# Loads of two rows, and half of the row sums with their halves added on TensorE

## The chip, the cores and the metric

The kernel runs on one core of one Trainium2 chip. The metric is the device time of an execution in microseconds. The times before are those of three runs.

## The reference

The input `x` has 32 x 512 rows of 1024 positive fp32 numbers, 67.1 MB in all. For each row the sum of the reciprocals is wanted:

```python
def reference(x: np.ndarray) -> np.ndarray:
    return np.sum(1.0 / x, axis=-1).astype(np.float32)
```

## The kernel before

The 16384 rows are laid out as 128 partitions with 128 rows each (`x_v`), so that "a row" below means one row in each of the 128 partitions: a tile of 128 x 1024 fp32, 512 KB. The kernel walks once over these 128 rows in loads of one to four rows, listed in `GROUPS`. An entry `(np_, ns, eng)` is one load with `np_` paired rows and `ns` single rows; `eng` is the engine that forms the products. All instructions are issued in the order of the list, and each engine works its own queue in that order. There is no planner.

A paired row is worked by its halves a and b, 512 elements each, with 1/a + 1/b = (a + b) / (a b):

- SyncE loads the rows of the group into `xt` (line 73). `xpool` has eight buffers of up to four rows.
- GpSimd multiplies the halves, `pr` = a b (line 75), for all paired rows of the load in one instruction. For the last row VectorE does it.
- ScalarE forms the reciprocal of the product as Exp(-Ln(S pr)) with S = 2^17: Ln in place in `pr` (line 85), and Exp into `rc` in PSUM (line 87), each for all paired rows in one instruction.
- VectorE multiplies the whole row of 1024 by `rc`, which is read twice through a broadcast, and sums into one column of `sums` (line 90), one instruction for each row. The sum of both products is S (a + b) / (S a b).

A single row (the `ns` rows) needs no product: ScalarE takes Ln and Exp(-Ln) of all 1024 elements with a running sum (lines 77 and 78), and neither GpSimd nor VectorE touches it. The list before has 112 paired and 16 single rows: two loads of two rows, then fifteen loads of `(3, 1)` alternating with fourteen of `(4, 0)`, two loads of two rows, and four of one.

When VectorE has read the last row of a load, its `xt` buffer is free, and SyncE may issue the load eight places further on. `pr` has four buffers, `rc` two. At the end `sums` goes out in one transfer (line 103). TensorE does nothing in this kernel.

Of the kernel before, what the change touches and what calls it, by code (L numbers as in the profile page):

```python
# [1 line left out]

# [5 lines left out]


@with_exitstack  # L10
def kernel(
    ctx: ExitStack,
    tc: tile.TileContext,
    x: bass.AP,
    out: bass.AP,
):

    nc = tc.nc
    f32 = mybir.dt.float32
    P = 128
    D = 1024
    H = D // 2
    F = 128

    S = float(2**17)


    GP, DV = nc.gpsimd, nc.vector
    GROUPS = (
        [(1, 1, GP), (2, 0, GP)]
        + [(3, 1, GP), (4, 0, GP)] * 14
        + [(3, 1, GP), (2, 0, GP), (2, 0, GP)]
        + [(1, 0, GP), (1, 0, GP), (1, 0, GP), (1, 0, DV)]
    )  # L40

    Ln = mybir.ActivationFunctionType.Ln
    Exp = mybir.ActivationFunctionType.Exp
    mult = mybir.AluOpType.mult
    add = mybir.AluOpType.add

    x_v = x.flatten_outer_dims().rearrange("(p f) d -> p f d", p=P)
    out_v = out.flatten().rearrange("(p f) -> p f", p=P)

    act_sets = list(get_activation_tables(nc.m.arch).keys())  # L50
    nc.scalar.add_instruction(  # L51
        mybir.InstLoadActFuncSet(
            name=nc.get_next_instruction_name(),
            act_func_set_id=act_sets.index("natural_log_exp_and_others"),
            ins=[],
            outs=[],
        )
    )

    xpool = ctx.enter_context(tc.tile_pool(name="xpool", bufs=8))  # L60
    ppool = ctx.enter_context(tc.tile_pool(name="ppool", bufs=4))
    opool = ctx.enter_context(tc.tile_pool(name="opool", bufs=1))
    rpool = ctx.enter_context(
        tc.tile_pool(name="rpool", bufs=2, space=bass.MemoryType.PSUM)
    )

    sums = opool.tile([P, F], f32)

    c0 = 0
    for np_, ns, eng in GROUPS:  # L70
        n = np_ + ns
        xt = xpool.tile([P, n, D], f32, tag="xt")
        nc.sync.dma_start(out=xt, in_=x_v[:, c0 : c0 + n, :])
        pr = ppool.tile([P, np_, H], f32, tag="pr")
        eng.tensor_tensor(out=pr, in0=xt[:, :np_, :H], in1=xt[:, :np_, H:], op=mult)  # L75
        for j in range(np_, n):
            nc.scalar.activation(out=xt[:, j, :], in_=xt[:, j, :], func=Ln)  # L77
            nc.scalar.activation(  # L78
                out=xt[:, j, :],
                in_=xt[:, j, :],  # L80
                func=Exp,
                scale=-1.0,
                accum_out=sums[:, c0 + j : c0 + j + 1],
            )
        nc.scalar.activation(out=pr, in_=pr, func=Ln, scale=S)  # L85
        rc = rpool.tile([P, np_, H], f32, tag="rc")
        nc.scalar.activation(out=rc, in_=pr, func=Exp, scale=-1.0)  # L87
        for j in range(np_):
            row = xt[:, j, :].rearrange("p (h e) -> p h e", h=2)
            nc.vector.tensor_tensor_reduce(  # L90
                out=row,
                in0=row,
                in1=rc[:, j, :].unsqueeze(1).to_broadcast([P, 2, H]),
                scale=S,
                scalar=0.0,
                op0=mult,
                op1=add,
                accum_out=sums[:, c0 + j : c0 + j + 1],
            )
        c0 += n  # L100
    assert c0 == F, c0

    nc.sync.dma_start(out=out_v, in_=sums)


# [1 line left out]
_INS = ['x']  # L107
_OUTS = [((32, 512), 'float32')]


# [23 lines left out]
```

## Time and profile before

| | |
|---|---|
| median of three runs | 179.79 us (179.39 to 180.21) |
| profiled execution | 180.0 us |
| its span, first to last instruction | 178.2 us |
| VectorE busy | 131.3 us, 74% |
| ScalarE busy | 142.9 us, 80% |
| GpSimd busy | 127.4 us, 71% |
| read from HBM | 67.11 MB |

The profile is one execution. PE is TensorE, DVE is VectorE, ACT is ScalarE, POOL is GpSimd, SP is SyncE; `L75` is line 75 of the kernel. A row of a group gives the line, the engine, the operation, output and input by their names in the program, their shape, the count, and then the busy time in us, the mean of one instruction in ns, and the idle time of the engine just before them with what ended it. A row of the timeline gives start and duration in us. Rows of slices divide the span into forty equal parts, with the busy share in tenths, and 9 for 90% and more.

### The profile page before, as it was taken

The numbers are of one execution on the slowest core, as the hardware profiler recorded it, in microseconds if no ns is written. First come the engines' busy times: TensorE is split into PE (matmuls) and PEld (weight loads), VectorE is DVE, ScalarE is ACT, GpSimd is POOL, SyncE is SP. The second block draws the span as 40 slices with busy tenths as digits, with TensorE's granted clock in tenths as the row PEclk, the third lists the DMA queues.
The fourth block names the chain that finished last, engine by engine and source line by source line (L and its number), as shares of the span: only waits on it lengthen the run. The fifth ranks groups of instructions, "written<-read, shape, count | busy, mean of one in ns | idle before, by whom it ended". The sixth has DMA issues, their size and how long they took to land. (4 is left out here: it accounts for less than half of the span.)

```text
span 178.2 us, 617 instructions
## 1 busy us (share of the span) xinstructions
DVE 131.3 (74%) x225; ACT 142.9 (80%) x123; POOL 127.4 (71%) x40
## 2 busy tenths in 40 slices
DVE  0043629749697987979797979879797979799982
ACT  2757399396998979797979989797979799899531
POOL 0446946959789696969697896969696978998000
DMA  5999899999999999999999999999999999991000
GB/s 202 445 416 430 349 423 438 412 416 430 449 416 416 450 423 416 434 439 419 416 449 427 416 430 445 419 416 449 427 416 421 452 416 414 409 365 66 0 0 15
DMA packets 5477, 67.22 MB, mean 377 GB/s; under 512 B 608, under 2 KB 736, under 8 KB 1248
## 3 DMA queue, kind: packets, MB, share of 16 engines
q1 hardware_dynamic: 5472, 67.18, 89.8%
q14 instruction: 5, 0.04, 0.1%
HBM read 67.11 MB, written 0.07 MB: 377 GB/s over the span
## 5 line engine op out<-in xcount | busy, mean ns | idle before, releaser
L90 DVE CUSTOM_DVE_ANT_1 xt<-xt,rc 128x1024 f32<-128x1024 f32 x112 | 130.4, 1218 | 44.4 <-POOL pr L75 18.8
L75 POOL TENSOR_TENSOR pr<-xt 128x1536 f32<-128x1536 f32 (+3 forms) x36 | 127.2, 3540 | 36.6 <-DMA xt<-in_x_dram 36.6
L85 ACT ACTIVATE pr<-pr 128x1536 f32<-128x1536 f32 (+3 forms) x37 | 54.9, 1486 | 22.8 <-POOL pr L75 20.6
L87 ACT ACTIVATE rc<-pr 128x1536 f32<-128x1536 f32 (+3 forms) x37 | 54.3, 1467 | 3.6 <-DVE sums L90 2.6
L77 ACT ACTIVATE xt<-xt 128x1024 f32<-128x1024 f32 x16 | 16.7, 1042 | 3.9 <-DMA xt<-in_x_dram 3.9
L78 ACT ACTIVATE xt<-xt 128x1024 f32<-128x1024 f32 x16 | 16.9, 1057 | 0.5
L90 DVE DVE_READ_ACCUMULATOR2_ANT sums<- 128x1 f32 x112 | 9.2, 82 | 0.0
L78 ACT ACTIVATION_READ_ACCUMULATOR xt<-xt 128x1 f32 x16 | 3.0, 186 | 0.0
L51 ACT ACT_TABLE_LOAD x1 | 1.3, 1283 | 0.7 <-PEq L118 0.7
L75 DVE TENSOR_TENSOR pr<-xt 128x512 f32<-128x512 f32 x1 | 0.7, 684 | 0.0
L118 POOL MEMSET const-float32-0.0<- 128x1 f32 x1 | 0.1, 98 | 0.2 <-issue 0.2
L118 POOL MEMSET const-bfloat16-1.0<- 128x1 bf16 x1 | 0.1, 101 | 0.0
L118 POOL MEMSET const-uint8-127<- 128x1 uint8 x1 | 0.1, 101 | 0.0
L118 POOL MEMSET const-float32-1.0<- 128x1 f32 x1 | 0.1, 98 | 0.0
## 6 DMA issues: line engine op xcount, KB each, us to landing
xt<-in_x_dram SPq DMA_DIRECT2D x29, 2048.0 KB, 26.7
xt<-in_x_dram SPq DMA_DIRECT2D x4, 1024.0 KB, 14.6
xt<-in_x_dram SPq DMA_DIRECT2D x4, 512.0 KB, 12.8
out_dram<-sums SPq DMA_DIRECT2D x1, 64.0 KB, 1.5
```

The source lines that it names most:

```text
L51: nc.scalar.add_instruction(mybir.InstLoadActFuncSet(name=nc.get_next_instruction_name(), act_func_set_id=act_sets.index("natural_log_exp_ ...
L75: eng.tensor_tensor(out=pr, in0=xt[:, :np_, :H], in1=xt[:, :np_, H:], op=mult)
L77: nc.scalar.activation(out=xt[:, j, :], in_=xt[:, j, :], func=Ln)
L78: nc.scalar.activation(out=xt[:, j, :], in_=xt[:, j, :], func=Exp, scale=-1.0, accum_out=sums[:, c0 + j : c0 + j + 1],)
L85: nc.scalar.activation(out=pr, in_=pr, func=Ln, scale=S)
L87: nc.scalar.activation(out=rc, in_=pr, func=Exp, scale=-1.0)
L90: nc.vector.tensor_tensor_reduce(out=row, in0=row, in1=rc[:, j, :].unsqueeze(1).to_broadcast([P, 2, H]), scale=S, scalar=0.0, op0=mult, op ...
L118: nc = _bacc.Bacc("TRN2", target_bir_lowering=False, num_devices=1)
```

## The change

There is a fourth field in the list's entries, `on_pe`. Loads have two rows at most, and `xpool` has sixteen buffers of two rows in place of eight of four: the same 128 KB in each partition.

For a load with `on_pe`, TensorE forms a + b: two fp32 matmuls for each row, with an identity as the stationary operand and the two halves as the moving ones, accumulated in a PSUM tile `sm` (two buffers). ScalarE's Exp then writes back into `pr` in SBUF instead of into a PSUM tile, and VectorE multiplies 512 elements of `pr` by 512 of `sm` and sums, instead of 1024 by a broadcast of 512. The identity is made once on GpSimd (a memset and a select) ahead of the loop.

The list has kinds A (two paired rows as before), B (two paired rows, halves added on TensorE) and C (one paired row, one single row). There are 24 loads of A, 30 of B, 7 of C and six loads of one row, four of them with `on_pe`; 7 rows instead of 16 go through ScalarE alone.

```diff
-    GROUPS = (
-        [(1, 1, GP), (2, 0, GP)]
-        + [(3, 1, GP), (4, 0, GP)] * 14
-        + [(3, 1, GP), (2, 0, GP), (2, 0, GP)]
-        + [(1, 0, GP), (1, 0, GP), (1, 0, GP), (1, 0, DV)]
+    A, B, C = (2, 0, GP, False), (2, 0, GP, True), (1, 1, GP, False)
+    GROUPS = (
+        [A, B, A, B, C, B, A, B] * 7
+        + [A, B, A, B, A]
+        + [(1, 0, GP, True), (1, 0, GP, False)] * 2
+        + [(1, 0, GP, True), (1, 0, DV, True)]
     )
...
-    xpool = ctx.enter_context(tc.tile_pool(name="xpool", bufs=8))
+    xpool = ctx.enter_context(tc.tile_pool(name="xpool", bufs=16))
...
+    spool = ctx.enter_context(
+        tc.tile_pool(name="spool", bufs=2, space=bass.MemoryType.PSUM)
+    )
     sums = opool.tile([P, F], f32)
+    ident = opool.tile([P, P], f32)
+    make_identity(nc, ident)
...
         eng.tensor_tensor(out=pr, in0=xt[:, :np_, :H], in1=xt[:, :np_, H:], op=mult)
+        if on_pe:
+            sm = spool.tile([P, np_, H], f32, tag="sm")
+            for j in range(np_):
+                for h in range(2):
+                    nc.tensor.matmul(
+                        sm[:, j, :],
+                        lhsT=ident,
+                        rhs=xt[:, j, h * H : (h + 1) * H],
+                        start=h == 0,
+                        stop=h == 1,
+                    )
...
-        rc = rpool.tile([P, np_, H], f32, tag="rc")
+        if on_pe:
+            rc = pr
+        else:
+            rc = rpool.tile([P, np_, H], f32, tag="rc")
         nc.scalar.activation(out=rc, in_=pr, func=Exp, scale=-1.0)
         for j in range(np_):
-            row = xt[:, j, :].rearrange("p (h e) -> p h e", h=2)
+            if on_pe:
+                row, rec = rc[:, j, :], sm[:, j, :]
+            else:
+                row = xt[:, j, :].rearrange("p (h e) -> p h e", h=2)
+                rec = rc[:, j, :].unsqueeze(1).to_broadcast([P, 2, H])
             nc.vector.tensor_tensor_reduce(
                 out=row,
                 in0=row,
-                in1=rc[:, j, :].unsqueeze(1).to_broadcast([P, 2, H]),
+                in1=rec,
```

More of the change, by code (lines that the diff above doesn't have):

```diff
@@ L7 @@
 from concourse.hw_specs import get_activation_tables
+from concourse.masks import make_identity
 @with_exitstack
@@ L65 @@
     )
+    spool = ctx.enter_context(
+        tc.tile_pool(name="spool", bufs=2, space=bass.MemoryType.PSUM)
+    )
     sums = opool.tile([P, F], f32)
+    ident = opool.tile([P, P], f32)
+    make_identity(nc, ident)
     c0 = 0
-    for np_, ns, eng in GROUPS:
+    for np_, ns, eng, on_pe in GROUPS:
         n = np_ + ns
```

## The prediction

> **What bounds the kernel now.** I read the page's busy shares and slices first, then the waits (the engines' and the load queue's own), then the load landings on GpSimd's line, and last the end of the run in windows and instruction by instruction.
>
> ```profile
> span 178.2 us, 617 instructions
> DVE 131.3 (74%) x225; ACT 142.9 (80%) x123; POOL 127.4 (71%) x40
> ...
> DMA  5999899999999999999999999999999999991000
> ...
> POOL pr L75 <- DMA xt<-in_x_dram: 36.6, 31, 5.1
> SPq L73 <- DVE sums L90: 137.5, 29, 7.6
> ```
>
> No compute engine is full. The DMA row is full from the second slice to the 36th and then empty, and 31 of GpSimd's 36 products waited for a load. SyncE does wait 137.5 us for buffers, but the DMA row has no hole, so those waits are early enough. So two pieces set the time: a stream of loads up to about 162 us, and what is left to compute behind it.
>
> The stream's pace is read where GpSimd was idle until a load landed, since it then starts at the landing:
>
> ```profile
> 5.57 1.27 POOL L75 TENSOR_TENSOR pr<-xt 128x512 f32<-128x512 f32 x1 [5.13 <-DMA xt<-in_x_dram]
> 8.04 2.35 POOL L75 TENSOR_TENSOR pr<-xt 128x1024 f32<-128x1024 f32 x1 [1.20 <-DMA xt<-in_x_dram]
> 12.93 3.44 POOL L75 TENSOR_TENSOR pr<-xt 128x1536 f32<-128x1536 f32 x1 [2.54 <-DMA xt<-in_x_dram]
> 17.83 4.51 POOL L75 TENSOR_TENSOR pr<-xt 128x2048 f32<-128x2048 f32 x1 [1.45 <-DMA xt<-in_x_dram]
> 24.70 3.45 POOL L75 TENSOR_TENSOR pr<-xt 128x1536 f32<-128x1536 f32 x1 [2.37 <-DMA xt<-in_x_dram]
> ...
> 142.60 3.45 POOL L75 TENSOR_TENSOR pr<-xt 128x1536 f32<-128x1536 f32 x1 [0.36 <-DMA xt<-in_x_dram]
> 147.50 4.54 POOL L75 TENSOR_TENSOR pr<-xt 128x2048 f32<-128x2048 f32 x1 [1.45 <-DMA xt<-in_x_dram]
> ```
>
> A four-row load takes 4.90 us (12.93 to 17.83, and 142.60 to 147.50); the one two-row load that can be read takes 2.47 (5.57 to 8.04). One interval is longer: 17.83 to 24.70 is 6.87, a stall of 1.97 us that the windows show too, as a drop of the rate:
>
> ```profile
> 17.00:18.00 1.00, 0.00 (x0) 0.97 (x2) 0.17 (x1) 1.00 1.95 393
> 18.00:19.00 1.00, 0.00 (x0) 1.00 (x1) 1.00 (x1) 1.00 0.53 229
> 19.00:20.00 1.00, 0.51 (x1) 0.37 (x1) 1.00 (x1) 1.00 0.69 295
> ...
> 100.00:150.00 50.00, 41.88 (x73) 44.74 (x37) 40.98 (x11) 1.00 1.01 428
> 156.00:173.20 17.20, 16.76 (x29) 12.30 (x16) 8.23 (x5) 1.00 0.27 109
> 161.00:162.00 1.00, 0.97 (x1) 0.97 (x2) 1.00 (x2) 1.00 0.37 152
> 162.00:163.00 1.00, 1.00 (x3) 1.00 (x2) 0.95 (x1) 1.00 0.02 8
> ```
>
> (Columns: window, VectorE, ScalarE and GpSimd busy with instruction counts, TensorE's granted clock, DMA share, GB/s.) The loads are over at 162, but the end is 13.7 us later, and in that stretch VectorE is full: 16.76 of 17.20 us. It does fifteen rows one behind the other, a row each 1.14 us, and then one short chain for the last row:
>
> ```profile
> 156.01 1.22 DVE L90 CUSTOM_DVE_ANT_1 xt<-xt,rc 128x1024 f32<-128x1024 f32 x1 [1.26 <-POOL pr L75]
> 157.16 1.22 DVE L90 CUSTOM_DVE_ANT_1 xt<-xt,rc 128x1024 f32<-128x1024 f32 x1
> ...
> 172.45 0.68 DVE L75 TENSOR_TENSOR pr<-xt 128x512 f32<-128x512 f32 x1
> 173.16 0.63 ACT L85 ACTIVATE pr<-pr 128x512 f32<-128x512 f32 x1 [2.23 <-DVE pr L75]
> 173.82 0.60 ACT L87 ACTIVATE rc<-pr 128x512 f32<-128x512 f32 x1
> 174.46 1.22 DVE L90 CUSTOM_DVE_ANT_1 xt<-xt,rc 128x1024 f32<-128x1024 f32 x1 [1.33 <-ACT rc L87]
> 175.72 0.35 SPq L103 DMA_DIRECT2D out_dram<-sums  x1
> ```
>
> VectorE is the bound of the last 14 us alone; before that its work is free.
>
> **The change part by part.** Prices of one instruction, by shape:
>
> ```profile
> L90 DVE CUSTOM_DVE_ANT_1 xt<-xt,rc 128x1024 f32<-128x1024 f32 x112 | 130.4, 1218 | 44.4 <-POOL pr L75 18.8 <-issue 15.2 <-ACT rc L87 10.4
> L78 ACT ACTIVATE xt<-xt 128x1024 f32<-128x1024 f32 x16 | 16.9, 1057 | 0.5
> L77 ACT ACTIVATE xt<-xt 128x1024 f32<-128x1024 f32 x16 | 16.7, 1042 | 3.9 <-DMA xt<-in_x_dram 3.9
> L75 POOL TENSOR_TENSOR pr<-xt 128x1024 f32<-128x1024 f32 x3 | 7.1, 2371 | 1.2 <-DMA xt<-in_x_dram 1.2
> L75 POOL TENSOR_TENSOR pr<-xt 128x512 f32<-128x512 f32 x4 | 5.1, 1282 | 5.2 <-DMA xt<-in_x_dram 5.1
> L85 ACT ACTIVATE pr<-pr 128x1024 f32<-128x1024 f32 x3 | 3.1, 1046 | 1.5 <-POOL pr L75 1.5
> L87 ACT ACTIVATE rc<-pr 128x1024 f32<-128x1024 f32 x3 | 3.1, 1027 | 0.3 <-DVE sums L90 0.2
> L85 ACT ACTIVATE pr<-pr 128x512 f32<-128x512 f32 x5 | 3.1, 616 | 2.2 <-DVE pr L75 2.2
> L87 ACT ACTIVATE rc<-pr 128x512 f32<-128x512 f32 x5 | 3.0, 601 | 2.4 <-DVE sums L90 2.4
> L78 ACT ACTIVATION_READ_ACCUMULATOR xt<-xt 128x1 f32 x16 | 3.0, 186 | 0.0
> L75 DVE TENSOR_TENSOR pr<-xt 128x512 f32<-128x512 f32 x1 | 0.7, 684 | 0.0
> L73 SPq DMA_DIRECT2D xt<-in_x_dram x37: 327/328/700, 0.7 to 154.9; - x37
> ```
>
> *The new mix.* 24 loads of kind A (two rows, as before), 30 of B (two rows, halves summed on TensorE), 7 of C (one product row, one row wholly on ScalarE) and six single rows, four of them on TensorE: 67 loads, 64 rows on TensorE, 57 full rows and 64 half rows on VectorE, 7 rows wholly on ScalarE instead of 16.
>
> *Eight loads, sixteen rows, in the steady part.* The stream brings them in 8 x 2.47 = 19.8 us. GpSimd needs 7 x 2.371 + 1.282 = 17.9. ScalarE needs 2.07 for an A, 2.09 for a B (its Exp now goes to SBUF, which I price like the Ln there, 1.046), 3.4 to 3.5 for a C; 3 x 2.07 + 4 x 2.09 + 3.5 = 18.1, with gaps of 0.03 between them 18.5. VectorE needs 7 x 1.14 + 8 x 0.60 = 12.8. A half row is between half of 1.218 and the 0.684 that another 512-element pass takes; I take 0.68 alone and 0.60 as the step in a row, for the same 0.08 overlap that makes 1.14 of 1.22. So all three stay under the stream: GpSimd at 90%, ScalarE at 93%.
>
> *The loads.* 61 of two rows and six of one. The price of halving them is 2.47 against 2.45 for half of 4.90, so 60 x 0.02 = 1.2 us; from below nothing, if 2.45 holds. SyncE issues 30 more times 0.33 us, 10 us of an engine that waits 137.5. The buffers hold 32 rows, as before. A B's buffer comes free when GpSimd and TensorE have read it, earlier than now, since VectorE no longer reads it.
>
> *TensorE.* 128 matmuls of 512 columns, and no row of this trace has one. The nearest are the other engines' passes over 512 elements: 0.601 (ScalarE into PSUM) to 1.282 (GpSimd). A B comes each 4.94 us and brings four matmuls, so there is room for 1.235 each; the low end hides, the high end would just become the pace. I take the low row, since ScalarE's pass, like a matmul, streams one operand from SBUF into PSUM; any price below 1.235 gives the same sum. The cover is that a B's product must go through GpSimd and ScalarE first (2.37 + 2.1 us).
>
> The Trainium skill, in "FP8 and Floating Point Precision", says that true fp32 is four passes through the array, and "TensorE: Matmul & The Clock Gate", Back-to-back issue gap and Part 1, gives 215.7 ns for one pass of 512 columns at the full clock and 426.7 at the half clock that is the idle state. By it my estimate is 0.86 us for a matmul at the full clock, which hides as well, and 1.71 at the half clock, which does not (the first rival); no row here can show it.
>
> *New waits.* VectorE's half row waits for TensorE besides ScalarE; behind it wait the next load's rows, and VectorE has 7 us to spare in 19.8. The B's result stays in its `pr` buffer until VectorE is done, so GpSimd's product four loads later waits for VectorE: a load lives 2.37 + 2.1 + 1.2 = 5.7 us and its buffer is wanted after 4 x 2.47 = 9.9, so this costs nothing; if the lag grew by 4 us, GpSimd would stall. TensorE waits for VectorE two B's back, 9.9 us: the same cover.
>
> *The identity.* Two GpSimd instructions, before the first load lands at 5.57; even at two passes of 1.282 they end in time, and the first B lands at 8.04.
>
> *The sum.* Last two-row load: 5.57 + 60 x 2.47 + 2.0 for the stall = 155.8 (the long stretch from 24.70 to 142.60, 24 loads of 4.91, holds no second stall of that size). Then GpSimd 2.37 (158.2), ScalarE 2.1 (160.3). Five single rows follow; their loads land each 1.2, GpSimd needs 1.28 and ScalarE 0.616 + 0.601 + 0.03 = 1.25, so ScalarE ends at 160.3 + 5 x 1.25 = 166.5. The last row's product waits on VectorE behind the half row before it: 0.6 (167.1), product 0.7 (167.8), Ln and Exp 1.30 as from 173.16 to 174.46 (169.1), half row 0.7 (169.8). Out behind it, 178.2 - 175.72 = 2.5: a span of 172.3. The profiled execution took 180.0 for its span of 178.2, so 1.8 more: 174.1. Its 180.0 lies 0.2 above the median 179.79 of the runs; 173.9 is my number. Against before: the loads end about 1 us later, the rest behind them falls from 13.7 to about 7.
>
> **The rivals.**
>
> *TensorE sets the pace (the slower side).* One mechanism: a matmul of t over 1.235 us, through the rate at which TensorE takes fp32 or a granted clock below 1. Then the last half row ends at 8.04 + 128 t + 0.7, and the time, with the 4.3 behind it less 0.2, is 12.8 + 128 t: 176.9 at GpSimd's 1.282, the same as before at 1.305, 205 at 1.5. For it: nothing in the rows excludes it, and the granted clock of 1.00 in the windows is that of a TensorE that does nothing. Against: the nearest streaming row is half of that, and a TensorE that falls behind is continuously busy. By the Trainium skill's half-clock estimate above it would be 232; the same page, Part 1, says that about 3.4 us of sustained work lift the clock, so that a lagging TensorE would speed up, which no run here shows yet. Chance 0.10: 0.02 faster, 0.01 same, 0.07 slower.
>
> *Smaller loads are slower.* Each 0.01 us over 2.47 costs 0.6 us: at 2.54 it is 178.1, at 2.57 no change, and at the slowest full slice of the page, 349 GB/s or 3.00 us for 1.05 MB, 206. Against: the read 2.47, itself two-row loads back to back.
>
> ```profile
> GB/s 202 445 416 430 349 423 438 412 416 430 449 416 416 450 423 416 434 439 419 416 449 427 416 430 445 419 416 449 427 416 421 452 416 414 409 365 66 0 0 15
> ```
>
> The Trainium skill's page "SBUF — State Buffer", The DMA setup-cost knee, speaks against the change: about 2 us fixed for each transfer, 341 GB/s at 1 MiB. My estimate by it is 3.07 us for a load and a time near 210; the landings at 5.57 and 8.04 disagree for loads queued behind each other. Chance 0.07: 0.03 faster, 0.01 same, 0.03 slower.
>
> *ScalarE or GpSimd eats the gain.* They have 1.3 and 1.9 us of room in 19.8. If each ScalarE instruction cost 0.1 more (16 and some in eight loads), ScalarE would need 20.2 and the end move by 0.4 x 7.6 = 3, with ten such instructions behind the last two-row load 4: 177.9. Chance 0.08: 0.05 faster, 0.03 same.
>
> *The stall is not the kernel's and does not come back.* The loads end 2 us earlier: 171.9; with 2.45 for a load 170.7. It is part of the forecast's own range.
>
> **How the numbers follow.** The forecast has 0.75, with a range of its own of 170.7 to 177, all faster. A change under 0.5% (178.9 to 180.7) can't be told from none. Faster: 0.75 + 0.02 + 0.03 + 0.05 = 0.85; same 0.01 + 0.01 + 0.03 = 0.05; slower 0.07 + 0.03 = 0.10. The range is 170.7 to 178.6: from no stall and 2.45 a load to just over ScalarE's case, leaving out the slow ends of the first two rivals.
>
> **What would show it.** DMA row full to about 161 to 164 us; half rows on VectorE of 0.60 to 0.69; GpSimd and ScalarE each near 90% in the steady part, still waiting for loads; in the last stretch ScalarE full and VectorE with holes. Wrong if VectorE's main wait is TensorE with matmuls over 1.2 us, if landings of two rows are over 2.5 apart, or if GpSimd waits for VectorE.

## The result, and the profile after

The changed kernel takes 175.16 us (median of four, 174.57 to 175.67) against 179.63 for the kernel before in the same runs: a ratio of 0.9745, 95% interval 0.970 to 0.979. The forecast was 173.9, in a range of 170.7 to 178.6. The profiled execution took 174.78 us for a span of 172.6, so 2.2 outside the span where I had 1.8. Against 173.9 the median is 1.3 us late: 0.3 in the span, 0.4 outside it, and 0.6 because the median lies 0.4 above the profiled execution where I had put it 0.2 below. One experiment below (TensorE with the old loads) has times from 180.42 to 184.32 us; its time and ratio are those of its five shorter executions, and its profile is of a longer one (184.19).

The page after, its busy shares, slices and waits (engine, line, what it waited for, us in total, times, longest):

```profile
span 172.6 us, 1342 instructions
PE 120.9 (70%) x256; PEld 47.4 (27%) x256; DVE 109.8 (64%) x243; ACT 142.0 (82%) x156; POOL 143.4 (83%) x72
...
DMA  5999999999999999999999999999999999999500
...
POOL pr L85 <- DMA xt<-in_x_dram: 15.2, 15, 4.3
...
PE sm L90 <- DVE sums L118: 1.9, 1, 1.9
SPq L83 <- DMA xt<-in_x_dram: 123.4, 59, 2.6
```

The stream is as full as before, and reaches one slice further, in slices of 4.3 us and not 4.5. GpSimd still waits for loads, but 15 times and not 31: it has nearly become as slow as the stream. SyncE no longer waits for VectorE but for the landing of an earlier load.

Prices of the new instructions, by shape, and the landings where GpSimd or TensorE waited for them:

```profile
L90 PE MATMUL sm<-xt,ident 128*128 128x512 f32 x256 | 120.9, 617 | 47.0 <-DMA xt<-in_x_dram 45.0 <-DVE sums L118 1.9
L118 DVE CUSTOM_DVE_ANT_0 pr<-pr,sm 128x512 f32<-128x512 f32 x64 | 41.6, 685 | 9.8 <-ACT pr L111 8.6
L85 POOL TENSOR_TENSOR pr<-xt 128x1024 f32<-128x1024 f32 x54 | 127.6, 2365 | 20.3 <-DMA xt<-in_x_dram 15.0 <-ACT pr L106 1.1
...
5.58 2.34 POOL L85 TENSOR_TENSOR pr<-xt 128x1024 f32<-128x1024 f32 x1 [4.27 <-DMA xt<-in_x_dram]
8.46 7.35 POOL L85 TENSOR_TENSOR pr<-xt 128x1024 f32<-128x1024 f32 x3 [0.55 <-DMA xt<-in_x_dram]
18.48 18.66 POOL L85 TENSOR_TENSOR pr<-xt 128x1024 f32<-128x1024 f32 x8 [1.21 <-DMA xt<-in_x_dram]
38.39 9.79 POOL L85 TENSOR_TENSOR pr<-xt 128x1024 f32<-128x1024 f32 x4 [1.25 <-DMA xt<-in_x_dram]
48.69 8.72 POOL L85 TENSOR_TENSOR pr<-xt 128x1024 f32<-128x1024 f32 x4 [0.51 <-DMA xt<-in_x_dram]
8.53 9.04 PE L90 MATMUL sm<-xt,ident 128*128 128x512 f32 x16 [8.53 <-DMA xt<-in_x_dram]
98.39 3.67 PE L90 MATMUL sm<-xt,ident 128*128 128x512 f32 x8 [1.29 <-DMA xt<-in_x_dram]
104.30 8.80 PE L90 MATMUL sm<-xt,ident 128*128 128x512 f32 x16 [2.25 <-DMA xt<-in_x_dram]
```

Eight two-row loads take 19.91 us (18.48 to 38.39), 2.489 each. The stall of 1.97 us is not there; smaller ones are: 2.88 for the second load, 10.30 for four loads from 38.39, 5.91 for two from 98.39, together 0.4 + 0.3 + 0.9 over the pace of 2.489; what causes them is open. The profile shows two records for each fp32 matmul (256 for 128).

The end, instruction by instruction:

```profile
158.93 1.06 ACT L106 ACTIVATE pr<-pr 128x1024 f32<-128x1024 f32 x1 [0.33 <-POOL pr L85]
165.90 1.22 DVE L118 CUSTOM_DVE_ANT_1 xt<-xt,rc 128x1024 f32<-128x1024 f32 x1
166.36 0.63 ACT L111 ACTIVATE pr<-pr 128x512 f32<-128x512 f32 x1
167.04 0.69 DVE L85 TENSOR_TENSOR pr<-xt 128x512 f32<-128x512 f32 x1
167.65 0.68 DVE L118 CUSTOM_DVE_ANT_0 pr<-pr,sm 128x512 f32<-128x512 f32 x1
167.77 0.63 ACT L106 ACTIVATE pr<-pr 128x512 f32<-128x512 f32 x1 [0.78 <-DVE pr L85]
169.09 0.69 DVE L118 CUSTOM_DVE_ANT_0 pr<-pr,sm 128x512 f32<-128x512 f32 x1 [0.75 <-ACT pr L111]
169.81 0.35 SPq L131 DMA_DIRECT2D out_dram<-sums  x1
```

ScalarE takes the last two-row load at 158.93 (forecast 158.2), ends the fifth single row at 166.99 (166.5), and the last half row ends at 169.8 (169.8). VectorE is full from 161.18 to 168.33, which the forecast, with ScalarE full and VectorE with holes, did not have.

### The profile page after: what moved, and what is told of

It reads as the page before. It is cut to its first block, busy times and chain, and to the rows that moved or that the text cites. A ratio compares the mean times of both kernels' runs of the same rounds, so it can differ in the third digit from the quotient of the medians.

```text
span 172.6 us, 1342 instructions
## 1 busy us (share of the span) xinstructions
PE 120.9 (70%) x256; PEld 47.4 (27%) x256; DVE 109.8 (64%) x243; ACT 142.0 (82%) x156; POOL 143.4 (83%) x72
## 4 chain that ended last, share of the span: by engine, by line
DMA 78%; POOL 11%; ACT 2%; issue 2%; DVE 2%; SPq 1%; PE 1%; POOLq 0%; DVEq 0%
DMA xt<-in_x_dram 78%; POOL pr L85 11%; SPq L83 1%; ACT pr L106 1%; PE sm L90 1%; DVE xt L118 1%; ACT rc L111 1%; DVE pr L118 0%; ACT pr L111 0%; DVE pr L85 0%; POOLq L85 0%; DVE sums L118 0%; DVEq L118 0%; DVEq L157 0%
## 5 line engine op out<-in xcount | busy, mean ns | idle before, releaser
L85 POOL TENSOR_TENSOR pr<-xt 128x1024 f32<-128x1024 f32 (+1 forms) x66 | 142.7, 2166 | 21.1 <-DMA xt<-in_x_dram 15.2
L90 PE MATMUL sm<-xt,ident 128*128 128x512 f32 x256 | 120.9, 617 | 47.0 <-DMA xt<-in_x_dram 45.0
L118 DVE CUSTOM_DVE_ANT_1 xt<-xt,rc 128x1024 f32<-128x1024 f32 x57 | 67.7, 1219 | 50.2 <-issue 27.2
L106 ACT ACTIVATE pr<-pr 128x1024 f32<-128x1024 f32 (+1 forms) x67 | 65.0, 970 | 24.5 <-POOL pr L85 23.7
L90 PEld LDWEIGHTS sm<-xt,ident 128*128 128x128 f32 x256 | 47.4, 195 | 119.7 <-issue 57.8
L118 DVE CUSTOM_DVE_ANT_0 pr<-pr,sm 128x512 f32<-128x512 f32 x64 | 41.6, 685 | 9.8 <-ACT pr L111 8.6
L111 ACT ACTIVATE pr<-pr 128x1024 f32<-128x1024 f32 (+1 forms) x34 | 34.2, 1006 | 1.0
L111 ACT ACTIVATE rc<-pr 128x1024 f32<-128x1024 f32 (+1 forms) x33 | 29.9, 906 | 0.8
L118 DVE DVE_READ_ACCUMULATOR2_ANT sums<- 128x1 f32 x121 | 10.0, 82 | 0.0
L99 ACT ACTIVATE xt<-xt 128x1024 f32<-128x1024 f32 x7 | 7.3, 1041 | 0.0
L98 ACT ACTIVATE xt<-xt 128x1024 f32<-128x1024 f32 x7 | 7.3, 1040 | 0.0
L99 ACT ACTIVATION_READ_ACCUMULATOR xt<-xt 128x1 f32 x7 | 1.3, 186 | 0.0
## 6 DMA issues: line engine op xcount, KB each, us to landing
xt<-in_x_dram SPq DMA_DIRECT2D x61, 1024.0 KB, 19.8
```

Of the source, the lines that this page charges most:

```text
L90: nc.tensor.matmul(sm[:, j, :], lhsT=ident, rhs=xt[:, j, h * H : (h + 1) * H], start=h == 0, stop=h == 1,)
L118: nc.vector.tensor_tensor_reduce(out=row, in0=row, in1=rec, scale=S, scalar=0.0, op0=mult, op1=add, accum_out=sums[:, c0 + j : c0 + j + 1],)
```

## The experiments

Ratios are to the kernel before, timed beside each run. The two theories at the outset: A, the finer cut carries the gain; B, TensorE's shorter sums carry it.

**The cut without TensorE.** Edit, in the list:

```diff
+    GROUPS = [(a, b, e, False) for a, b, e, _ in GROUPS]
```

> The changed kernel's loads and chains of two rows, but no load uses TensorE: all 121 paired rows are full rows of 1.14 us on VectorE. Theory A (the finer cut carries the gain): VectorE needs 15 x 1.14 = 17.1 us for sixteen rows that arrive in 8 x 2.49 = 19.9, so no backlog forms before the end; behind the last two-row load it trails ScalarE by one row, and the end moves by about 0.54 for the half row ahead of the last product and 0.54 for the last row: 1 to 1.5 us over the changed kernel, 176.2 to 176.7. Theory B (the shorter sums on TensorE carry it, as the forecast's sum had it in its tail): VectorE's rows pile up at the end again as before, 178.5 to 179.8.

Measured: 176.89 us, 0.983 (0.981 to 0.986), 0.2 over what theory A gave. Of the 4.5 us of the change, about 3.0 come without any matmul. (With the cut go the chains of two and 7 instead of 16 rows on ScalarE alone; a run below that has both of these, but not the small loads, gains 0.7.)

**TensorE without the cut.** The list before, TensorE on 64 rows. Each of the two buffers of `sm` holds one row of sums here and not two, beside two buffers of up to three rows for `rc`.

```diff
+        [(1, 1, GP, False), A]
+        + [(3, 1, GP, False), (4, 0, GP, True)] * 14
+        + [(3, 1, GP, False), B, B]
+        + [(1, 0, GP, True)] * 3 + [(1, 0, DV, True)]
...
+                sm = spool.tile([P, H], f32, tag="sm")
```

> The kernel before with its loads of four rows and eight buffers, and TensorE's sums on the fourteen (4, 0) loads, the last two loads of two rows and all four single rows at the end: 64 rows, as many as in the changed kernel. Theory A, the cut alone: no gain, 178.5 to 179.8. Theory B, the sums alone: the whole gain, 175.2. Stepped through with the rows of before: ScalarE still ends the (3, 1) load's Exp at 160.9; then three full rows on VectorE to 164.4, ScalarE's two pairs and three single rows to 168.8, product, chain and half row to 172.1: 176.2, which would mean that each of the two alone brings most of the gain and that they do not add.

Measured: 181.46 us, 1.009 (1.005 to 1.013): a little slower, which no theory gave. The waits, a window near the end, and the last half rows of VectorE:

```profile
DVE pr L120 <- PE sm L92: 53.2, 34, 3.3
PE sm L92 <- DVE sums L120: 31.8, 15, 3.1
...
157.00:167.00 10.00, 10.00 (x16) 4.00 (x16) 4.52 (x11) 9.28 (x11) 5.86 (x4) 0.70 0.36 144
...
177.47 0.69 DVE L120 CUSTOM_DVE_ANT_0 pr<-pr,sm 128x512 f32<-128x512 f32 x1 [1.02 <-PE sm L92]
179.19 0.69 DVE L120 CUSTOM_DVE_ANT_0 pr<-pr,sm 128x512 f32<-128x512 f32 x1 [1.02 <-PE sm L92]
```

(The window's columns are TensorE, weight loads, VectorE, ScalarE, GpSimd, granted clock, DMA share and GB/s.) In the profiled execution TensorE and VectorE, with two row buffers, wait for each other, 31.8 and 53.2 us, and the clock falls, to 0.70 in this window; how much of the 0.9% this explains is not shown. Even at its best a row takes TensorE 1.72 us (177.47 to 179.19), more than VectorE's full row of 1.14. So this run does not isolate the sums: it put all the last rows on the slower engine. At 1.72 us a row, where the stream brings one in 1.22 (4.90 for four), TensorE can't take every row.

**TensorE on the last eight loads alone.**

```diff
+    GROUPS = [(a, b, e, False) for a, b, e, _ in GROUPS[:-8]] + GROUPS[-8:]
```

> The changed kernel with TensorE's sums on its last eight loads alone (one B load and four single rows; every earlier B becomes an A). Theory A and the forecast (VectorE's work ahead of the tail is free): as the changed kernel, 174.6 to 175.7. Rival: the shorter sums in the steady part matter (VectorE's lag there delays buffers or ScalarE): as without TensorE, 176.2 or more.

Measured: 175.29 us, 0.976 (0.973 to 0.979), as the changed kernel. With small loads the sums on TensorE are worth 1.6 us, all of it at the end.

**Three matmuls for a row.**

```diff
-                for h in range(2):
+                for i, h in enumerate((0, 0, 1)):
...
-                        start=h == 0,
-                        stop=h == 1,
+                        start=i < 2,
+                        stop=i != 1,
```

> The changed kernel with one more matmul for each row on TensorE: the first half is written twice, the second writing starting the accumulation again, so the sums are the same. A matmul is two records of 0.46 us, 0.92 us; six for a load of two rows need 5.5 us where loads with them come every 4.97. The forecast's limit of 1.235 us for a matmul pair would then be passed, TensorE becomes the pace: 8.5 + 64 x 3 x 0.92 = 184.7, and with 5 behind it 189 to 191. Rival (a matmul costs less when TensorE is never idle, or the wait is hidden by ScalarE's chain): under 180.

Measured: 180.69 us, 1.005 (1.003 to 1.008). TensorE became the pace, but at a lower price than I had put:

```profile
PE 166.7 (93%) x384; PEld 73.5 (41%) x384; DVE 107.5 (60%) x243; ACT 142.3 (80%) x156; POOL 143.7 (81%) x72
...
8.17 166.72 PE L90 MATMUL sm<-xt,ident 128*128 128x512 f32 x384 [8.17 <-DMA xt<-in_x_dram]
```

One unbroken row of 384 records in 166.72 us is 0.434 for a record and 0.87 for a matmul. My 0.92 came from 3.67 us for eight records, which holds the run-out of the last one. By 0.87 three matmuls a row need 5.2 us for two rows of the 4.97 at hand, and the end follows: 8.2 + 166.7. The Trainium skill, "FP8 and Floating Point Precision" (true fp32 is four passes) with "TensorE: Matmul & The Clock Gate", Part 1 (215.7 ns for a pass of 512 columns), gave 0.86 as an estimate; this trace agrees.

**The fine cut at the end alone**, without TensorE:

```diff
-        + [(3, 1, GP), (4, 0, GP)] * 14
-        + [(3, 1, GP), (2, 0, GP), (2, 0, GP)]
-        + [(1, 0, GP), (1, 0, GP), (1, 0, GP), (1, 0, DV)]
+        + [(3, 1, GP), (4, 0, GP)] * 13
+        + [(2, 0, GP)] * 7
+        + [(1, 0, GP)] * 5
+        + [(1, 0, DV)]
```

> The kernel before without TensorE, its loads of four rows kept for the first 108 rows, and the last twenty cut as in the changed kernel: seven loads of two rows, six of one. Theory A1 (only the cut of the last loads matters, since only the tail is VectorE's): as the changed cut without TensorE or better by the faster stream of four-row loads, 175.5 to 176.9. Theory A2 (what counts is the lag with which VectorE comes into the tail, and full rows can't work it off): VectorE ends a four-row load 4.5 + 3.8 + 4.6 = 12.9 us after its landing, a two-row load 2.4 + 2.1 + 2.3 = 6.8; two full rows need 2.28 of the 2.49 between landings, so seven loads win back 1.5 us, and the end lies about 12 us behind the last landing: 178 to 179.

Measured: 179.63 us, 0.998 (0.996 to 1.000): no gain worth the name. VectorE's rows at the last four-row load, which landed at 137.51, and at the end:

```profile
137.51 23.25 POOL L76 TENSOR_TENSOR pr<-xt 128x2048 f32<-128x2048 f32 x10 [2.01 <-DMA xt<-in_x_dram]
...
146.02 1.22 DVE L91 CUSTOM_DVE_ANT_1 xt<-xt,rc 128x1024 f32<-128x1024 f32 x1 [1.82 <-issue]
147.17 1.22 DVE L91 CUSTOM_DVE_ANT_1 xt<-xt,rc 128x1024 f32<-128x1024 f32 x1
...
171.14 1.22 DVE L91 CUSTOM_DVE_ANT_1 xt<-xt,rc 128x1024 f32<-128x1024 f32 x1
172.28 0.69 DVE L76 TENSOR_TENSOR pr<-xt 128x512 f32<-128x512 f32 x1
```

From 146.02 to 172.28 VectorE does 23 rows without a hole, 1.14 each. It begins that load 8.5 us behind its landing and never catches up in the fine part. Its last loads were also issued late, the last two from 159.87 to 162.48, since SyncE waits for VectorE to free one of the eight buffers (143.2 us in 33 waits) and a one-row load takes one like any other. VectorE was full all the while, so that is not what set the end.

**Loads of four rows, chains of two** (pairs of loads of the changed kernel joined, up to the last eleven):

```diff
+        [[A], [B], [A, B], [C, B], [A, B]]
+        + [[A, B], [A, B], [C, B], [A, B]] * 6
+        + [[A], [B], [A], [B], [A]]
+        + [[(1, 0, GP, True)], [(1, 0, GP, False)]] * 2
+        + [[(1, 0, GP, True)], [(1, 0, DV, True)]]
```

> The changed kernel's chains of two rows and its order, TensorE's sums as there, but 27 pairs of loads joined: from the third chain on, one load of four rows feeds two chains, up to the last eleven loads, which stay at two rows and one row. Six buffers of four rows and eight of two. Theory (the stream's pace is that of the load's size: 2.486 us for two rows alone, 4.895 for four): 27 x (4.972 - 4.895) = 2.1 us less stream, chains as they are: 172.8 to 174.0. Rival 1: GpSimd, which needs 2.46 us for two rows with its gaps, is the pace by now and the stream's gain is lost: 174.6 to 175.5. Rival 2: coarser landings bring back the lag of before: over 176.

Measured: 173.99 us, 0.966 (0.963 to 0.970), the best of all. Where GpSimd waits for a landing, two loads of four rows take 9.79 us:

```profile
87.43 4.70 POOL L95 TENSOR_TENSOR pr<-xl 128x1024 f32<-128x1024 f32 x2 [0.49 <-DMA xl<-in_x_dram]
92.33 4.69 POOL L95 TENSOR_TENSOR pr<-xl 128x1024 f32<-128x1024 f32 x2 [0.19 <-DMA xl<-in_x_dram]
97.22 3.61 POOL L95 TENSOR_TENSOR pr<-xl 128x512 f32<-128x512 f32 x2 [0.20 <-DMA xl<-in_x_dram]
```

That is 2.448 for two rows against 2.489: the price of halving the loads, 1.7% of the stream. Of the 2.1 us it should bring, some 1 arrived.

**Ten buffers for sixteen.**

```diff
-    xpool = ctx.enter_context(tc.tile_pool(name="xpool", bufs=16))
+    xpool = ctx.enter_context(tc.tile_pool(name="xpool", bufs=10))
```

> The changed kernel with ten load buffers of two rows in place of sixteen. In its trace SyncE waits for the landing of an earlier load in 59 of 67 issues and a load takes 19.8 us from issue to landing, eight loads' worth: at most eight are on their way, whatever the buffers. Theory: a load lives about 7 us behind its landing, three loads' worth, so ten buffers leave seven on their way, 17 us of stream: no change, 174.6 to 175.7. Rival (the sixteen buffers carry part of the gain): over 176.5.

Measured: 174.86 us, 0.971 (0.968 to 0.974), as the changed kernel. SyncE's waits, and the loads' time from issue to landing (last column, first of the changed kernel, then here):

```profile
xt<-in_x_dram SPq DMA_DIRECT2D x61, 1024.0 KB, 19.8
```

```profile
SPq L83 <- DVE sums L118: 102.5, 29, 6.6
SPq L83 <- DMA xt<-in_x_dram: 21.9, 19, 2.4
...
xt<-in_x_dram SPq DMA_DIRECT2D x61, 1024.0 KB, 18.4
```

SyncE waits for VectorE again, 102.5 us, and each load is issued 1.4 us nearer to its landing, without an effect: whether there are ten buffers or sixteen is not what counts.

**Joined loads without TensorE, and with it on the last eight loads alone.** The list of the joined run with `False` in every load, and in all but the last eight.

> Loads of four rows with chains of two, as in the run with joined loads, but no load uses TensorE: VectorE takes full rows throughout, as before the change. What is left against the kernel before is the size of the chains (and 7 instead of 16 rows on ScalarE alone), and the cut of the last eleven loads, which by itself brought nothing. Theory (the size of the chains carries the gain): as with joined loads and TensorE, and 1.5 to 1.7 us more, the price of full rows in the tail: 175.3 to 175.9. Rival (the small loads of the body carry it, and TensorE made up for them in the joined run): 177.5 to 179.8.

> The joined loads with TensorE's sums on the last eight loads alone. Theory (TensorE is of use in the tail only): as with TensorE everywhere, 173.4 to 174.5. Rival (at a faster stream VectorE's 17.1 us of full rows for sixteen that arrive in 19.6 leave a lag that the tail inherits): 175 or more.

Measured: 179.03 us, 0.997 (0.995 to 0.998), and 175.91 us, 0.979 (0.977 to 0.982). Both rivals were right, and both my theories fell: that the size of the chains carries the gain, and that TensorE is of use in the tail only. With joined loads TensorE is worth 5.0 us (179.03 to 173.99), and 1.9 of them are lost if it helps at the end only. In windows up to the last product (columns VectorE, ScalarE, GpSimd, clock, DMA share, GB/s), and in a load of each, first the joined run without TensorE, then the small loads without it:

```profile
148.95:171.30 22.35, 22.35 (x39) 16.56 (x21) 15.68 (x10) 1.00 0.57 211
142.14 18.75 POOL L97 TENSOR_TENSOR pr<-xl 128x1024 f32<-128x1024 f32 x9 [1.30 <-DMA xl<-in_x_dram]
152.38 1.22 DVE L130 CUSTOM_DVE_ANT_1 xl<-xl,rc 128x1024 f32<-128x1024 f32 x1
```

```profile
148.95:168.90 19.95, 19.38 (x33) 15.93 (x20) 15.46 (x9) 1.00 0.65 265
138.89 9.81 POOL L87 TENSOR_TENSOR pr<-xt 128x1024 f32<-128x1024 f32 x4 [1.21 <-DMA xt<-in_x_dram]
144.76 1.22 DVE L120 CUSTOM_DVE_ANT_1 xt<-xt,rc 128x1024 f32<-128x1024 f32 x1
```

The joined load lands at 142.14, and VectorE ends its last row at 153.6, 11.5 us later, then is full to the end. The two-row load lands at 138.89 and is done at 146.0, 7.1 later. The second chain of a joined load waits for GpSimd and ScalarE to end the first, and VectorE, with 17.1 us of full rows for 19.6 us of stream, wins that back too slowly.

**Joined loads in the first half, small ones in the second, no TensorE.**

> No TensorE, chains of two rows, loads joined to four rows only in the first half (15 joined loads), then 24 and 5 loads of two rows and the six single ones. VectorE's full rows need 17.1 us of the 19.9 in which sixteen rows land, so the lag of four-row landings, some 4 us more than that of two-row ones, is worked off within two of these stretches, and the second half has three and more. Theory (it is VectorE's lag when it comes into the tail that sets the end): as small loads throughout without TensorE, less the stream's gain of 15 x 0.077 = 1.2: 175.4 to 176.9. Rival (four-row loads cost time wherever they stand, for another reason): halfway to 179.0 or more, 177.9 to 179.

Measured: 176.05 us, 0.979 (0.975 to 0.982), within the theory's range and 0.8 below small loads throughout. The same coarse loads that cost 2 us ahead of the tail cost nothing when VectorE has the second half to work off its lag. And the lag ahead of the tail is the short one: the two-row load that lands at 137.98 in this run is done on VectorE at 145.09, 7.1 us later, as with small loads throughout. So the lag at the end is the cause, not the loads' size as such.

## Why the prediction was right, and where not

- *The bound and the end.* Right in the main: the stream sets the time up to the end, and the last half row ended at 169.8 as forecast. But that this came out to 0.1 us is luck, since three errors cancelled. The landings were 0.7 late: a load takes 2.489 and not 2.47 (1.1 us over 60 loads), and the stalls came to 1.6 in pieces and not 2.0. GpSimd started the last two-row load at 156.52 and not 155.8 for this reason, not for its own speed: from 139 to 154 it starts each second product within 0.03 us of the landing for which TensorE waits (149.08 and 149.06, 154.06 and 154.03), and one load behind 154.03 is 156.52. ScalarE's single rows took 1.19 and not 1.25, which gave 0.3 back. And the forecast had the last product wait behind the half row of the fifth single row; VectorE did it at 167.04, ahead of that half row (167.65), which gave back the rest. In the run with TensorE on the last eight loads alone VectorE did the two in the forecast's order, the product at 167.47. GpSimd was mis-sized, 2.37 a load for 2.47 with the gaps between its instructions (18.66 us for the eight from 18.48, where I had 17.9), but stayed under the stream's 19.91.
- *The half rows.* 0.685 alone, 0.61 in a row: as taken.
- *TensorE.* 0.87 us a matmul, not the 0.60 that I took; under the limit of 1.235, so the sum did not change. The limit itself is shown by the run with three. The half-clock rival did come up, in two places. TensorE's first sixteen records, from 8.53, take 9.04 us, and sixteen at the later pace take 7.13 (in the run with the old loads); the granted clock reads 1 there all the same. And TensorE idled from 102.06 to 104.30 behind a late load, and the windows read

```profile
102.00:104.00 2.00, 0.06 (x1) 0.00 (x0) 1.26 (x5) 1.79 (x2) 1.23 (x1) 1.00 0.98 406
104.00:106.00 2.00, 1.70 (x3) 0.77 (x4) 0.88 (x3) 1.34 (x2) 1.68 (x1) 0.65 1.01 418
106.00:108.00 2.00, 2.00 (x4) 0.88 (x3) 1.88 (x4) 1.26 (x2) 1.88 (x2) 0.50 1.02 426
108.00:110.00 2.00, 2.00 (x6) 0.82 (x5) 0.19 (x1) 1.66 (x2) 1.84 (x2) 1.00 0.98 410
```

  The granted clock was 0.50 from 104.6 on, and back at 1 at 108.0, after 3.7 us of work. As the forecast held, a TensorE that lags is busy and so regains its clock. The Trainium skill, "TensorE: Matmul & The Clock Gate", Part 1, puts the return at about 3.4 us of sustained work, which agrees, and the fall behind an idle window of about 3.4 us, which does not: the pause here was 2.25.
- *Smaller loads.* 2.489 against 2.448: the rival's mechanism exists at 1.7%. The rule of the Trainium skill's page "SBUF — State Buffer", The DMA setup-cost knee (3.07 us by my estimate), does not hold for loads queued behind each other.
- *What was wrong* is the step "VectorE is the bound of the last 14 us alone; before that its work is free", and with it the reading that the shorter sums alone shrink the tail. The tail of before was VectorE's lag behind four-row landings, carried in from the body. The last four-row load of before, which landed at 147.50, was done on VectorE at 160.7, 13.2 us later:

```profile
159.44 1.22 DVE L90 CUSTOM_DVE_ANT_1 xt<-xt,rc 128x1024 f32<-128x1024 f32 x1
```

  (The prediction counts fifteen rows one behind the other in that stretch; there are fourteen, with a hole of 0.36 us behind this one, and the last row follows alone.) The cut alone, with the chains of two that go with it, is worth 3.0 us of the 4.5; the sums alone, on joined loads, are worth 5.0. Both lessen what VectorE has left when the stream ends, and they do not add. The finer cut does it by less lag coming in (7.1 us for 11.5), the cheaper rows by working the lag off on the way: with joined loads and TensorE the last four-row load, which lands at 141.94, is done at 152.3, still 10.4 later, but at 159.5 VectorE waits again.
- *The new waits* cost nothing in the body, as said. At the end TensorE waited 1.9 us once for VectorE, since single rows come too fast for its two buffers; whether that cost anything was not tried.

## What to carry to other kernels

An engine at 80 to 90% in a stream-bound body is not free work: what counts is how far behind a landing it is when the stream ends, and whether it has the room to work that off before. Take a load shortly ahead of the end and read how long behind its landing the engine is done with it: 13.2 us in the kernel before, 7.1 with two-row loads. Where the engine then has next to no holes up to the end, a cheaper instruction in that stretch moves the end (TensorE on the last eight loads alone). Finer landings must begin early enough for the lag to be worked off: from the second half on they did it, for the last 20 rows alone they brought nothing. Run each of two edits made together with and without the other: here the sums were worth 5.0 us with joined loads and 1.7 with small ones, and the small loads gained 2.1 without the sums and cost 1.2 with them. (These are differences of medians; from the ratios they come out 0.1 to 0.4 us different.)

## What the runs showed of the hardware

- An fp32 matmul of 512 columns is two records of 0.434 us, 0.87 in all, and a row's sum of two takes 1.72: longer than the same row whole on VectorE (1.14).
- TensorE's granted clock fell to 0.50 after a pause of 2.25 us in the changed kernel and after one of 1.89 with ten buffers (the last eight records then took 5.40 us and not 3.73). It stayed at 1 after pauses of 1.3 us between B loads, and after one of 2.89 with the old loads (sixteen records in 7.13 us). So the length of a pause alone does not decide it.
- TensorE starts slow: its first sixteen records take 9.04 us in the changed kernel, 9.21 with joined loads, 8.57 with ten buffers, and 9.03 where they begin only at 153.87 (the last eight loads alone), against 7.13 at the later pace. The granted clock reads 1 in the changed kernel all the while.
- GpSimd leaves 0.1 us between its products; its 83% busy share stood for 94% of the stream's pace (18.66 of 19.91).
- With sixteen buffers SyncE waited for a landing in 59 issues: about eight loads were on their way, 19.8 us from issue to landing by the page. Whether the chip or the program's own waits set this was not tried.
